# The low parts of the keys stacked twice, so that every score product contracts over 128 rows

## The chip, the cores and the metric

The kernel runs on one core of a Trainium2 chip, as one launch. The metric is the device time of one execution in microseconds. An execution's time is a little longer than its span in the trace, which goes from the first to the last instruction that was profiled.

## What is computed

The reference is two transformer blocks of two layers each, on 512 tokens of 1024 features, all in float32. The first block's layers have causal attentions with heads of 64 and a gated feed-forward; the second block's layers merge three branches (a global "axial" attention, a pooling branch and a neighbourhood attention) by gates, and have a feed-forward too. What the change touches is the product of queries and keys of the heads of 64:

```
s = q @ k.T / sqrt(64) + bias         # causal pairs, and both maps of the differential attention
s = [q_nope | q_rope] @ [k_nope | k_rope].T / sqrt(192)      # latent attention, rotated part of 64
s = einsum('bqhd,brqjhd->bhqrj', q_row, k_nb) + rpb          # neighbourhood attention
p = softmax(s);  o = p @ v
```

## The kernel before

Every float32 operand of a large product is split exactly into a high and a low part of a narrower type, and a product is summed from three: low times high, high times low, high times high (`mm3`, L356 to L360, nearly all of TensorE's work; the weights come from DRAM in chunks of 128x1024, through `Stream`).

For heads of 64 the split is arranged otherwise. Two heads lie in one tile, one in partitions 0 to 63 and one in 64 to 127. `stack` (L366) copies halves about by DMA, so that each head has one query tile with its high part above its low part, and one key tile with the high part of the keys in both halves. The low part of the keys stays as it was, one tile with a head in each half. `stacked` (L382) then gives two products per score tile: the query's high half times the low keys, which contracts over 64 rows (this text calls it a low product), and the whole query tile times the doubled high keys, which contracts over 128 rows:

```
        r = slice(64 * hd, 64 * hd + 64)
        q, kh, kl = store[hd], store[2 + hd], store[4]
        return [(q[r, c], kl[r, w]), (q[:, c], kh[:, w])]
```

`products` (L362, L364) issues them. They are used by the four pairs of causal heads and the four differential heads of the first layer ("even"), the four pairs and the rotated part of four latent heads of the second layer ("odd"), and the four pairs of the neighbourhood attention in each of the two layers of the second block. The axial attention has its own products (L1813, L1814), both over 128 rows, since its low keys are stored twice already.

Attention is a pipeline of units, a unit being at most a bank of scores: score products, then VectorE's sum with the bias and maximum (L629), ScalarE's exponential (L631), VectorE's scaling (L640, L642), TensorE's transposes (L654; L1832 in the neighbourhood attention), a copy, and the products with the values. `weave` (L531) mixes these units with dense work (projections, gates), and the framework then orders each engine's instructions by its own estimates; the order of the built program is fixed. All the tiles of 128x512 come from 42 blocks in SBUF. Guards on the number of free blocks hold work back: a neighbourhood unit is ready only with 6 free blocks (L1799), a gate of the last merge waits for 6 (L1660).

All the copies of `stack` and nearly all weight loads are issued from SyncE's queue, in order. A stack with keys issues six copies (three for the keys, three for the queries); the copy that overwrites a half waits there until the copies that read it have landed.

Of the kernel before, what the change touches and what calls it, by code (L numbers as in the profile page):

```python
# [10 lines left out]
F32R = mybir.dt.float32r  # L11
# [15 lines left out]
# the order of work in the pooling branch: gates, projections, mixing, products with the branch's weights  # L27
# [4 lines left out]
# ---------------------------------------------------------------- host layout  # L32
# [4 lines left out]
def weight_plan(I):  # L37
    """The weights in the order of their use: (key, scale, [128, n <= 1024])."""
# [145 lines left out]
def constants():  # L184
    """Arrays that follow from the shapes alone."""
    C = {}
    C["ident"] = np.eye(P, dtype=np.float32)
    # relative bias by reversed distance: column i stands for the distance 511 - i
# [35 lines left out]
    # pooling windows: 1 / count at the first and last eight tokens  # L224
# [5 lines left out]
    # neighbourhood windows, queries reversed within the tile: p = (15 - i) * 8 + (7 - r)  # L230
# [13 lines left out]
def rpb_layout(rpb):  # L244
    """[2, 8, 15, 31] as [2, 8, 16 shifts, 15 rows, 32 columns], zeros outside."""
    wide = np.zeros(rpb.shape[:3] + (48,), rpb.dtype)
    wide[..., 8:39] = rpb
    return np.ascontiguousarray(np.stack([wide[..., i:i + 32] for i in range(16)], axis=2))


# -------------------------------------------------------------------- program
class Blocks:
    """Slots of one size, handed out oldest-free first."""
# [19 lines left out]
class Stream:  # L273
    """Weights from DRAM, split exactly into two float32r parts some chunks ahead of their use."""
# [51 lines left out]
class Kernel:  # L326
# [8 lines left out]
    # ---- tiles  # L335
# [4 lines left out]
    def dbank(self):  # L340
        """A bank for dense work, in turn."""
# [13 lines left out]
    # ---- pieces  # L355
# [10 lines left out]
    def stack(self, qh, ql, kh=None, kl=None):  # L366
        """Two heads of 64, parts one above the other: per head, queries [high; low] and keys [high; high]."""
# [3 lines left out]
        if kh is not None:  # L371
            kb = self.blk.get(F32R)
            dma(kb[h], kh[g])
            dma(kb[g], kh[g])
            dma(kh[g], kh[h])
# [4 lines left out]
        return [qh, qb] if kh is None else [qh, qb, kh, kb, kl]  # L380

    def stacked(self, store, hd, c, w):  # L382
        r = slice(64 * hd, 64 * hd + 64)
        q, kh, kl = store[hd], store[2 + hd], store[4]
        return [(q[r, c], kl[r, w]), (q[:, c], kh[:, w])]

    def split(self, hi, lo, src):
        """src (float32, SBUF or PSUM) as the exact sum of two float32r parts."""
# [17 lines left out]
    # ---- pre-norm into the transposed, split hT  # L406
# [1506 lines left out]
```

## Time and profile before

| | before |
|---|---|
| time, median of 3 runs | 2935.75 us (2934.86 to 2935.95) |
| span of the profiled execution | 2933.1 us |
| around the span, from the median | 2.65 us |
| TensorE busy | 2878.6 us, 98% of the span, 13612 products |
| VectorE, ScalarE, GpSimdE busy | 1556.7, 1117.1, 125.2 us |
| DMA, mean of 16 engines | q1 (SyncE's and ScalarE's issues) 29.1% |

The profiled execution has no time of its own beside its span, so 2933.1 + 2.65 us stands for it, which is the median. Products are pipelined: two products of 512 columns start some 0.23 us apart though each is shown 0.39 us long, so a stretch is read by the starts, not by the busy time. A weight load (PEld) normally starts while the product before it streams.

### The profile page before, as it was taken

How to read it: one execution, taken by the hardware profiler on the slowest of the kernel's cores; microseconds unless marked ns; L12 is line 12 of the kernel's file. 1: busy time of each engine (PE TensorE's matmuls, PEld its weight loads, DVE VectorE, ACT ScalarE, POOL GpSimd, SP SyncE). 2: the span in 40 equal slices, each digit the busy share in tenths (PEclk: the TensorE clock that was granted, in tenths of full speed). 3: DMA queues.
4: the chain of work that ended last, by engine and by line, in shares of the span. 5: the costliest groups of instructions: out<-in, count | busy, mean ns of one | idle time of the engine just before them, and what ended most of it. 6: DMA issues, size and time to landing. Idle time of an engine off the chain costs nothing.

```text
span 2933.1 us, 34799 instructions
## 1 busy us (share of the span) xinstructions
PE 2878.6 (98%) x13612; PEld 2320.2 (79%) x13612; DVE 1556.7 (53%) x2673; ACT 1117.1 (38%) x1928; POOL 125.2 (4%) x206
## 2 busy tenths in 40 slices
PE   7999999999999999989999999999989999999999
PEld 6677888887678888777777888888867777888887
DVE  4566444335655443367556466652585554666533
ACT  3444333223433332234433344441444434444422
POOL 1000000000000000031000010000130000100000
PEclk9999999999999999999999999999999999999999
DMA  4432322333313223222223222233212222232232
GB/s 164 120 103 76 102 95 99 102 104 106 97 51 115 100 97 104 77 83 84 74 92 106 90 99 94 95 107 104 88 64 74 90 93 91 89 113 94 100 97 76
DMA packets 88849, 279.30 MB, mean 95 GB/s; under 512 B 11584, under 2 KB 14528, under 8 KB 88686
## 3 DMA queue, kind: packets, MB, share of 16 engines
q1 hardware_dynamic: 87726, 275.32, 29.1%
q8 instruction: 107, 1.75, 0.2%
q10 hardware_dynamic: 864, 1.64, 0.2%
q14 instruction: 56, 0.46, 0.0%
q0 software_dynamic: 96, 0.14, 0.0%
HBM read 258.38 MB, written 2.15 MB: 89 GB/s over the span
## 4 chain that ended last, share of the span: by engine, by line
PE 68%; issue 23%; DVE 5%; POOL 2%; DMA 1%; ACT 1%; SPq 0%; POOLq 0%; DVEq 0%; ACTq 0%
PE b L358 20%; PE b L359 20%; PE b L360 20%; PE b L364 2%; POOL s L403 1%; PE b L654 1%; PE b L1529 1%; DMA wr<-in_w_dram 1%; DVE k L1469 1%; PE b L1784 1%; POOL s L402 0%; PE b L1832 0%; PE b L1813 0%; DVE wl L301 0%; PE b L801 0%
## 5 line engine op out<-in xcount | busy, mean ns | idle before, releaser
L358 PE MATMUL b<-hh,wl 128*128 128x512 f32 (+1 forms) x2368 | 907.0, 384 | 1.8 <-ACT hh L389 1.0
L360 PE MATMUL b<-hh,wh 128*128 128x512 f32 (+1 forms) x2368 | 899.5, 380 | 0.0
L359 PE MATMUL b<-hl,wh 128*128 128x512 f32 (+1 forms) x2368 | 898.8, 380 | 0.0
L301 DVE TENSOR_TENSOR wl<-wr,wh 128x1024 fp32r<-128x1024 f32 (+1 forms) x407 | 495.9, 1221 | 530.8 <-ACT wh L300 529.0
L300 ACT CAST wh<-wr 128x1024 fp32r<-128x1024 f32 (+1 forms) x421 | 438.8, 1044 | 481.9 <-PE b L360 419.5
L358 PEld LDWEIGHTS b<-hh,wl 128*128 128x128 f32 x2368 | 446.1, 189 | 90.2 <-issue 10.6
L360 PEld LDWEIGHTS b<-hh,wh 128*128 128x128 f32 x2368 | 446.6, 189 | 83.4 <-issue 0.9
L359 PEld LDWEIGHTS b<-hl,wh 128*128 128x128 f32 x2368 | 447.1, 189 | 81.0 <-issue 3.2
L358 PE MATMUL b<-wh,k 128*128 128x512 f32 x900 | 352.9, 392 | 0.0
L359 PE MATMUL b<-wl,k 128*128 128x512 f32 x900 | 350.9, 390 | 0.0
L360 PE MATMUL b<-wh,k 128*128 128x512 f32 x900 | 350.5, 390 | 0.0
L358 PEld LDWEIGHTS b<-wh,k 128*128 128x128 f32 x900 | 169.1, 188 | 35.9 <-issue 0.8
L360 PEld LDWEIGHTS b<-wh,k 128*128 128x128 f32 x900 | 169.0, 188 | 35.6
L359 PEld LDWEIGHTS b<-wl,k 128*128 128x128 f32 x900 | 169.1, 188 | 33.9
L364 PE MATMUL b<-k,k 64*128 64x256 f32 (+9 forms) x400 | 128.3, 381 | 1.1 <-DMA k<-k 0.6
L1230 ACT ACTIVATE e<-b,cols_sb 128x512 f32<-128x512 f32 x88 | 68.4, 777 | 153.6 <-PE b L360 153.6
L364 PEld LDWEIGHTS b<-k,k 128*128 128x128 f32 (+1 forms) x400 | 71.1, 186 | 65.5 <-issue 33.3
L1231 DVE SCALAR_TENSOR_TENSOR e<-b,cols_sb,e 128x511 f32<-128x511 f32 x88 | 65.7, 747 | 104.5 <-ACT e L1230 104.3
L1220 DVE SCALAR_TENSOR_TENSOR e<-b,cols_sb,e 128x511 f32<-128x511 f32 x44 | 33.0, 750 | 159.2 <-ACT e L1219 159.2
L631 ACT ACTIVATE k<-k,s 128x256 f32<-128x256 f32 (+4 forms) x144 | 75.3, 524 | 72.1 <-DVE s L629 58.1
L1219 ACT ACTIVATE e<-b,cols_sb 128x512 f32<-128x512 f32 x44 | 34.3, 780 | 177.9 <-PE b L360 177.9
L359 PE MATMUL b<-wl,hh 128*128 128x512 f32 (+2 forms) x256 | 92.8, 362 | 0.4 <-DVE wl L301 0.3
(192 smaller groups left out, 3122.0 us busy)
## 6 DMA issues: line engine op xcount, KB each, us to landing
wr<-in_w_dram SPq DMA_DIRECT2D x451, 512.0 KB, 3.5
k<-k SPq DMA_DIRECT2D x126, 128.0 KB, 2.3
k<-brev SPq DMA_DIRECT2D x20, 256.0 KB, 3.3
x<-in_x_dram SPq DMA_DIRECT2D x4, 512.0 KB, 7.3
k<-in_rpb_dram SPq DMA_DIRECT2D x16, 128.0 KB, 2.7
wr<-in_w_dram SPq DMA_DIRECT2D x4, 448.0 KB, 3.2
e<-in_ffn_norm_dram SPq DMA_DIRECT2D x2, 512.0 KB, 3.7
e<-in_norm_mix_pre_dram SPq DMA_DIRECT2D x2, 512.0 KB, 4.4
```

The costliest lines, as they stand in the source:

```text
L300: nc.scalar.copy(hi[:, :n], raw[:, :n])
L301: (nc.gpsimd if self.pool > 0 else nc.vector).tensor_sub(lo[:, :n], raw[:, :n], hi[:, :n].bitcast(F32))
L358: mm(out, sl, mh, start=start, stop=False)
L359: mm(out, sh, ml, start=False, stop=False)
L360: mm(out, sh, mh, start=False, stop=stop)
L364: self.nc.tensor.matmul(out, s, m, start=i == 0, stop=i == len(pairs) - 1)
L403: nc.gpsimd.tensor_tensor(r, a, self.mhalf[:, :w], op=ALU.pow)
L631: nc.scalar.activation(s[:, c], s[:, c], AF.Exp, bias=mx[:, i:i + 1], scale=-1.0, accum_out=sm[:, i:i + 1])
L1219: nc.scalar.activation(c, b, AF.Identity, bias=self.col(("cb",), m), scale=self.col(("cw", 2), m))
L1220: nc.vector.scalar_tensor_tensor(c[:, 1:], b[:, :S - 1], self.col(("cw", 1), m), c[:, 1:], op0=ALU.mult, op1=ALU.add)
L1230: nc.scalar.activation(y, b, AF.Identity, bias=self.col(("cb",), mm), scale=self.col(("cw", 1), mm))
L1231: nc.vector.scalar_tensor_tensor(y[:, 1:], b[:, :S - 1], self.col(("cw", 0), mm), y[:, 1:], op0=ALU.mult, op1=ALU.add)
```

## The change

`stack` doubles the low parts of the keys as it does the high parts: one more block and three more copies for each stack with keys. `stacked` then multiplies the whole query tile, high over low, with the doubled low keys; the low-times-low term that was left out before is now in the sum. The number of products, their columns and all work of VectorE and ScalarE stay. Two guards follow: the last merge's gates wait for 7 free blocks, and a neighbourhood unit needs 6 free blocks only for the first unit of a pair, 2 for the others. Comments were dropped, which moves the line numbers by 3 below `stack`: L369 becomes L370, L654 becomes L657, L1529 L1532, L1832 L1835; L358 to L364 stay.

```diff
     def stack(self, qh, ql, kh=None, kl=None):
         h, g = slice(0, 64), slice(64, P)
         dma = lambda o, i: self.nc.sync.dma_start(o.bitcast(F32), i.bitcast(F32))
         qb = self.blk.get(F32R)
-        if kh is not None:
-            kb = self.blk.get(F32R)
-            dma(kb[h], kh[g])
-            dma(kb[g], kh[g])
-            dma(kh[g], kh[h])
+        keys = []
+        for part in (kh, kl):
+            if part is not None:
+                kb = self.blk.get(F32R)
+                dma(kb[h], part[g])
+                dma(kb[g], part[g])
+                dma(part[g], part[h])
+                keys.append((part, kb))
         dma(qb[g], qh[g])
         dma(qb[h], ql[g])
         dma(qh[g], ql[h])
         self.blk.put(ql)
-        return [qh, qb] if kh is None else [qh, qb, kh, kb, kl]
+        return [qh, qb] + [z for pair in keys for z in pair]
 
     def stacked(self, store, hd, c, w):
-        r = slice(64 * hd, 64 * hd + 64)
-        q, kh, kl = store[hd], store[2 + hd], store[4]
-        return [(q[r, c], kl[r, w]), (q[:, c], kh[:, w])]
+        q, kh, kl = store[hd], store[2 + hd], store[4 + hd]
+        return [(q[:, c], kl[:, w]), (q[:, c], kh[:, w])]
...
-                rope = k.stacked(mla["r", h // 2] + [cT[3][0], cT[3][0], cT[3][1]], h % 2, c, slice(0, n))
+                rope = k.stacked(mla["r", h // 2] + [cT[3][0]] * 2 + [cT[3][1]] * 2, h % 2, c, slice(0, n))
...
-            while len(k.blk.free) < 6:
+            while len(k.blk.free) < 7:
                 yield NEED
             yield from self.gate(L, 2, m)
...
-                     lambda: p in store and len(k.blk.free) >= 6, begin, tail)
+                     lambda: p in store and len(k.blk.free) >= (2 if tb else 6), begin, tail)
```

The change also moves instructions. The rows below are the built programs' order, without any time. Names are tiles with their numbers, `b` a bank of PSUM, `k` a block, `hh`/`hl` the parts of the normed activations, `wh`/`wl` those of the weights; shapes are those of the output.

TensorE, second pair of heads of the first layer, before: the low products (keys `k_716`) of the first two score tiles stand 27 rows higher, and the full products (`k_715`, the high keys) come one dense product into the next weight chunk.

```order
L360 MATMUL b_78_806<-hh,wh_515 128x512
L358 MATMUL b_79_841<-hh,wl_559 128x512
L364 MATMUL b_64_740<-k_715,k_643 128x512
L364 MATMUL b_69_758<-k_715,k_643 128x128
L364 MATMUL b_69_758<-k_716,k_643 128x384
L364 MATMUL b_69_758<-k_715,k_643 128x384
L359 MATMUL b_79_841<-hl,wh_558 128x512
```

The same place after the change (low keys `k_720`, high keys `k_719`):

```order
L358 MATMUL b_79_849<-hh,wl_563 128x512
L359 MATMUL b_79_849<-hl,wh_562 128x512
L364 MATMUL b_64_748<-k_720,k_647 128x512
L364 MATMUL b_64_748<-k_719,k_647 128x512
L364 MATMUL b_69_766<-k_720,k_647 128x128
L364 MATMUL b_69_766<-k_719,k_647 128x128
L364 MATMUL b_69_766<-k_720,k_647 128x384
L364 MATMUL b_69_766<-k_719,k_647 128x384
L360 MATMUL b_79_849<-hh,wh_562 128x512
```

The low products no longer stand ahead of the copies: low and full products stand together, 11 dense products into the next chunk instead of one.

SyncE's queue, the key copies of that same pair, before (each copy is 64x512; `x2` is two alike, `brev` is the bias table, `wr` a weight chunk):

```order
L763 DMA k_943<-brev 128x512
L763 DMA k_945<-brev 128x512
L369 DMA k_720<-k_715 64x512 x2
L286 DMA wr_804<-in_w_dram 128x1024
L369 DMA k_715<-k_715 64x512
```

And after:

```order
L370 DMA k_724<-k_719 64x512 x2
L370 DMA k_728<-k_720 64x512 x2
L766 DMA k_955<-brev 128x512
L370 DMA k_719<-k_719 64x512
L286 DMA wr_812<-in_w_dram 128x1024
L370 DMA k_720<-k_720 64x512
```

Two more copies stand before the one that completes the high keys, and one more, behind a weight load, completes the low keys.

TensorE, first pair of the neighbourhood attention in the second block's first layer, before: the first unit's scores (bank `b_989`) stand among the last axial work, and only dense work follows; the second unit's scores come some 120 rows later.

```order
L364 MATMUL b_989_11421<-k_11327,k_11251 128x256
L359 MATMUL b_997_11471<-hl,wh_11113 128x512
L364 MATMUL b_989_11421<-k_11326,k_11251 128x256
L364 MATMUL b_989_11421<-k_11327,k_11251 128x256
L654 MATMUL b_987_11398<-ident_sb,k_11356 128x128 x4
L364 MATMUL b_989_11421<-k_11326,k_11251 128x256
L654 MATMUL b_992_11433<-ident_sb,k_11373 128x128 x4
L360 MATMUL b_997_11471<-hh,wh_11113 128x512
L358 MATMUL b_997_11471<-hh,wl_11114 128x512
```

After, from the third unit's last score products to the first unit's transposes (the other products of the first three units stand just above):

```order
L364 MATMUL b_999_11516<-k_11383,k_11378 128x256
L364 MATMUL b_999_11516<-k_11379,k_11378 128x256
L360 MATMUL b_1011_11589<-hh,wh_11161 128x512
L358 MATMUL b_1011_11589<-hh,wl_11162 128x512
L359 MATMUL b_1011_11589<-hl,wh_11161 128x512
L657 MATMUL b_997_11506<-ident_sb,k_11443 128x128 x4
L364 MATMUL b_1005_11553<-k_11383,k_11378 128x192
L364 MATMUL b_1005_11553<-k_11379,k_11378 128x192
L1835 MATMUL b_1003_11541<-ident_sb,k_11474 128x128 x2
```

With the loosened guard three units' score products follow one another, and the fourth's begin before the first unit's transposes (`b_1003`); three dense products stand between.

## Rows read from the trace of the kernel before

**Rows 1.** Span and granted TensorE clock of the core.

```profile
core 0: 2933.1 us, clock 0.996
```

**Rows 2.** The page: busy time of each engine, share of the span, instructions.

```profile
PE 2878.6 (98%) x13612; PEld 2320.2 (79%) x13612; DVE 1556.7 (53%) x2673; ACT 1117.1 (38%) x1928; POOL 125.2 (4%) x206
```

**Rows 3.** Windows: stretch; length, busy us (instructions) per engine, clock, DMA share, GB/s.

```profile
78.00:272.00 194.00, 191.90 (x887) 137.37 (x886) 117.96 (x344) 82.26 (x225) 4.84 (x8) 1.00 0.34 96
...
690.00:870.00 180.00, 179.88 (x827) 130.46 (x826) 109.01 (x287) 78.44 (x190) 1.50 (x4) 1.00 0.30 85
...
1340.00:1473.00 133.00, 130.03 (x629) 99.23 (x629) 87.14 (x177) 62.47 (x126) 1.13 (x2) 1.00 0.25 78
1473.00:1640.00 167.00, 166.91 (x833) 127.59 (x832) 86.13 (x212) 62.79 (x133) 0.00 (x0) 1.00 0.31 95
```

**Rows 4.** Groups by form, weight loads of the score products: busy, mean ns, idle before.

```profile
L364 PEld LDWEIGHTS b<-k,k 128*128 128x128 f32 x224 | 39.8, 188 | 24.5 <-issue 10.1 <-ACT wh L303 1.0 <-ACT e L397 0.9
L364 PEld LDWEIGHTS b<-k,k 64*128 64x128 f32 x176 | 31.3, 183 | 41.0 <-issue 23.2 <-DVE s L640 2.9 <-DVE s L629 2.2
```

**Rows 5.** Timeline of TensorE, one low product among dense ones: start, length, instruction.

```profile
1602.17 0.39 PE L360 MATMUL b<-hh,wh 128*128 128x512 f32 x1
1602.49 0.38 PE L364 MATMUL b<-k,k 64*128 64x256 f32 x1
1602.80 0.50 PE L358 MATMUL b<-hh,wl 128*128 128x512 f32 x1
1603.14 0.40 PE L359 MATMUL b<-hl,wh 128*128 128x512 f32 x1
```

**Rows 6.** Timeline of TensorE, low and full products in turn, twice.

```profile
1614.66 0.40 PE L360 MATMUL b<-hh,wh 128*128 128x512 f32 x1
1614.99 1.21 PE L364 MATMUL b<-k,k 64*128 64x192 f32 x4
...
1616.29 0.39 PE L359 MATMUL b<-hl,wh 128*128 128x512 f32 x1
```

**Rows 7.** Timeline of TensorE, dense products of 256 columns.

```profile
290.23 0.28 PE L358 MATMUL b<-hh,wl 128*128 128x256 f32 x1
290.35 0.28 PE L359 MATMUL b<-hl,wh 128*128 128x256 f32 x1
```

**Rows 8.** Timeline of TensorE, an axial unit's two score products among dense ones.

```profile
1350.27 0.39 PE L1813 MATMUL b<-k,k 128*128 128x512 f32 x1
...
1350.73 0.39 PE L358 MATMUL b<-k,wl 128*128 128x512 f32 x1
```

**Rows 9.** Timeline of TensorE, low products that follow one another.

```profile
78.76 0.55 PE L364 MATMUL b<-k,k 64*128 64x512 f32 x2
...
185.60 0.50 PE L364 MATMUL b<-k,k 64*128 64x512 f32 x2
186.03 0.50 PE L359 MATMUL b<-hl,wh 128*128 128x512 f32 x1
...
2420.95 0.47 PE L364 MATMUL b<-k,k 64*128 64x256 f32 x2
```

**Rows 10.** The copies of L369: issues, who waited, issue to landing.

```profile
L369 SPq DMA_DIRECT2D k<-k x126: 461/462/946, 72.5 to 2440.8; - x126
...
  PE b L364: 0.6, 1
...
DMA to landing us min/median/max: 2.2/2.3/4.9
```

**Rows 11.** Groups by form, 1473 to 1640 us: VectorE's and ScalarE's steps of a unit.

```profile
L629 DVE CUSTOM_DVE_ANT_0 k<-b,k 128x256 f32<-128x256 f32 x16 | 6.2, 423 | 9.0 <-PE b L364 9.0
...
L642 DVE TENSOR_SCALAR k<-k,s 128x256 f32<-128x256 f32 x16 | 4.9, 350 | 0.2
...
L631 ACT ACTIVATE k<-k,s 128x256 f32<-128x256 f32 x16 | 8.1, 505 | 7.0 <-DVE s L629 7.0
...
L631 ACT ACTIVATION_READ_ACCUMULATOR k<-k,s 128x1 f32 x32 | 6.0, 188 | 0.0
```

## The prediction

> **What bounds the kernel now.** I read the page first: TensorE is busy 98% of the span, the other engines 53% and less [rows 2], at a granted clock of 0.996, its upper level of 2.4 GHz [rows 1]. Then the windows of the stretches that hold the score products [rows 3]: TensorE is busy 191.90 of 194, 179.88 of 180 and 166.91 of 167 us there (the second block's other layer, 2313 to 2480 us, repeats the last), while VectorE has 118, 109 and 86 us. So what TensorE is spared there shortens the kernel, as long as VectorE, ScalarE and the copies follow. A busy share hides whether TensorE streams or stands in a change of mode, so next come the starts in the timeline.
>
> Dense products of 512 columns start 0.23 us apart, and an axial unit's two products over 128 rows among them cost nothing extra: 1350.27 to 1350.73 us is two starts of 0.23 [rows 8]. A product of 256 columns takes 0.12 [rows 7]. A low product, over 64 rows, does cost extra. In [rows 5] the dense product before it is followed after 0.32 us in place of 0.23, the low product of 256 columns after 0.31 in place of 0.12, the next dense one after 0.34. From 1602.17 to 1603.14 is 0.97 us, where 0.23 + 0.12 + 0.23 = 0.58 would do: 0.39 us for one excursion to 64 rows and back. In [rows 6] two excursions stand in 1614.66 to 1616.29 = 1.63 us; with 0.12 for each of the four short products (they have 192 columns, so this is rather too much) and 0.23 for the two dense ones, 0.94 would do: 0.69 for two, 0.345 each. The weight load shows the same thing: before a low product the loader stood idle 41.0 us over 176 of them, most of it named "issue", which is no wait for another engine [rows 4].
>
> **What the change removes.** All 176 low products [rows 4] get 128 rows. Nine of them directly follow another low product (the first such pair is at 78.76, the last at 2420.95 us [rows 9]) and share its excursion, so 167 excursions go. At 0.345 to 0.39 us that is 57.6 to 65.1; I take 0.37, between the two, for 61.8 us. The products that replace them have the same columns, and their weight loads of 128 rows took 188 ns against 183 [rows 4], beside a streaming product: nothing.
>
> The Trainium skill's page "TensorEngine Tiling (Array Packing)", Key Properties, says that changing the tiling mode drains TensorE. The page "TensorE: Matmul & The Clock Gate", Single matmul latency, gives a product that hides no drain (398+N)/2.4 ns, so 166 ns above its columns; an excursion has two changes, and by that estimate the sum would be 167 x 0.332 = 55.4 us instead of 61.8.
>
> **What it adds: copies.** Each of the 20 stacks with keys (8, 4, 4 and 4) issues three more copies on SyncE's queue. An issue takes 0.46 us and a copy lands 2.2 to 4.9 us after it [rows 10]. They move no work of another engine, but the first low product of a pair now needs them, and weight loads queue behind. The order puts that first product 11 dense products into the next weight chunk, where the first full product stood one in: ten more, 2.3 us. The longer chain is one more issue pair (0.92 us) ahead of the last copy, and that last copy itself 0.46 us after its twin: 1.4 us, so the 2.3 us cover it if landing stays usual. TensorE waited for these copies 0.6 us, once [rows 10]. I take 0.1 us per stack, 2 us; the bounds are 0 and, if the last copy lands at 4.9 instead of 2.3 each time, 20 x 2.6 = 52 us. Weight loads late by some 1 to 2 us reach nobody: TensorE reads a chunk for 24 x 0.23 = 5.5 us and several chunks are prepared ahead; if that cover went, each stack would cost those 2 us, 40 in all, and TensorE would wait for a `wh`.
>
> **What it moves: the neighbourhood units.** With the looser guard three units of a pair stand together in the program, and the first one's transposes come after 8 short products of the next two units (0.96 us at 0.12), three dense ones (0.69), five transposes (below 0.12 each, 0.6) and two short products (0.24): 2.5 us after its scores. Its own chain takes at least: a sum with maximum 0.42, two exponentials with their accumulator reads 2 x (0.505 + 0.188) = 1.39, two scalings 0.70 [rows 11]: 2.5 us, and the four sums of the next two units (1.7 us) may stand before the scalings on VectorE: 4.2. So the first transposes wait 0 to 1.7 us, and the values' products and all dense work wait behind them on TensorE. Such packs of three come about twice more in each layer. I take 3.5 us per layer, 7 in all; bounds 0 and 3 x 2 x 1.7 = 10.
>
> **What is late next.** Each unit loses two excursions (0.74 us) of TensorE time that covered VectorE's and ScalarE's steps. How much of that comes back as waits is best read where there are no excursions: the axial stretch, with 32 units, leaves TensorE idle 133 - 130.03 = 3.0 us [rows 3], 0.09 per unit. For the 72 units of the other three attentions (24, 12, 24 and 12) that gives 6.7; they stall a little already, so I take 5. Bounds 0 and 72 x 0.3 = 22.
>
> **The sum.** 61.8 - 2 - 7 - 5 = 47.8 us less. The profiled execution's 2933.1 us and 2.65 around it are 2935.75, which is the median, since the former has no other time of its own: 2888 us. Its own range: 65.1 with no new wait gives 2871, 57.6 less all moderate losses (20) gives 2898.
>
> **Rivals.**
> *The softmax chain takes the place of the drains.* If VectorE and ScalarE, not TensorE, pace the attention stretches, most of what is freed comes back: 72 units at 0.3 us and 10 us in the neighbourhood stretches leave 61.8 - 22 - 10 - 2 = 28 us, 2908. For it: VectorE's share in the first stretch would go from 118 of 194 to 118 of some 170 us, 69% [rows 3]. Against: the axial stretch ran at 87 of 133, 66%, almost without waits. 12%.
> *The copies decide: slower.* The place is the first score product of a pair on TensorE, behind the last copy of the low keys; dense work stands behind it in order. With the other losses of 12 us it decides from (61.8 - 12) / 20 = 2.5 us of wait per stack. One round trip of 2.3 us [rows 10] that nothing covers would not do; two, 4.6 us, would cost 92 us in all and give 2935.75 + 92 - 61.8 + 12 = 2978. Against: the order moved the products by 2.3 us, and the copies of all but a pair's first use lie far ahead. 4%.
> *Side by side no more.* Low products of two heads use different halves of the rows and can run together: at 185.60 us two of 512 columns take 0.43 us to the next start, hardly more than one [rows 9]. If half of the 176 were hidden so, 88 x 0.17 (between 0.12 and 0.23) = 15 us of the gain would go, 2903. But only 2 pairs of the trace start together; low and full products alternate elsewhere. 4%.
> The Trainium skill's "TensorEngine Tiling (Array Packing)", Overview, promises up to twofold speed from two row tiles when the contraction is 64 or less, and so speaks against widening it; the trace shows the effect, in two places.
> *The change doesn't do what it says.* The surcharge might hang not on the rows but on the interruption of dense work; then nothing is gained and the waits remain, 2936 to 2945. [Rows 8] speak against it: the axial products interrupt dense work too, for nothing. 4%.
> My forecast keeps 76%.
>
> **How the numbers follow.** The likeliest gives 2888. The range goes from its lower end, 2871, rounded to 2870, up to take in the third rival and half of the first: 2905; some 2 in 10 is left out. A change of 0.2%, 6 us, is about what a measurement of this kernel can tell from none. Faster: the forecast, the first and third rivals and what little of the last could still gain, 93%. Same: the last one's milder half, 3%. Slower: the copies, and the last with its waits, 4%.
>
> **What would show it.** In the profile after, L364 has no 64-row form; starts around a lone score product are 0.23 and its own columns apart; the four stretches are shorter, the first by about 60 x 0.37 = 22 us, each neighbourhood stretch by about 11 less its waits; the axial stretches and the dense ones keep their length. If a step is wrong, it shows as idle TensorE: before L364 named by a copy (copies), before L657 or L1835 named by VectorE (chain), near 1480 and 2320 us (packs). I would be wrong altogether if the starts around score products kept their 0.31 to 0.34 us.

## The result and the profile after

| | before | after |
|---|---|---|
| time, median | 2935.39 us (2934.86 to 2935.95, 4 runs) | 2901.32 us (2897.02 to 2904.21, 4 runs) |
| ratio, with its 95% interval | | 0.9882 (0.9869 to 0.9894) |
| profiled execution, span | 2933.1 us | 2899.27 us, span 2897.2 us |

The change makes the kernel 34 us faster. The forecast was 48 us less, 2888 us, and its range of 2870 to 2905 us holds the result. In four runs each, the time after scatters over 7 us and that of before over 1. One of the four executions of experiment 6 below took 7301.66 us and counts as slow, so its median is that of the three others (the later expectations use 2885, the median of all four).

The span with the mean granted clock, and then the page's line of busy times (busy us, share of the span, instructions), of the kernel after, to be read beside [rows 1] and [rows 2]:

```profile
core 0: 2897.2 us, clock 0.995
```

```profile
PE 2829.7 (98%) x13612; PEld 2313.4 (80%) x13612; DVE 1551.5 (54%) x2673; ACT 1111.5 (38%) x1928; POOL 124.8 (4%) x206
```

TensorE has as many products as before and is busy 48.9 us less. The span is only 35.9 us shorter, so 13 us came back as TensorE standing still. The windows show in which stretches (columns as in [rows 3]):

```profile
78.00:264.00 186.00, 181.12 (x922) 140.29 (x921) 122.58 (x352) 83.33 (x231) 6.99 (x12) 1.00 0.42 118
...
670.00:850.00 180.00, 177.06 (x878) 137.92 (x878) 113.31 (x293) 79.85 (x194) 2.23 (x6) 1.00 0.35 100
1313.00:1446.00 133.00, 130.11 (x620) 99.25 (x619) 84.02 (x167) 61.13 (x123) 1.13 (x2) 0.99 0.24 77
1446.00:1612.00 166.00, 162.95 (x860) 130.31 (x859) 89.66 (x224) 64.64 (x136) 0.00 (x0) 1.00 0.36 106
```

In [rows 3] TensorE was idle 2.1 us in the first of them and 0.1 in the second and the last; now it is idle 4.9, 2.9 and 3.0. The axial stretch, which has no stacked score products, has 2.9 us as against 3.0. What ended the idle time is told by the weight loads of the score products (columns as in [rows 4]):

```profile
L364 PEld LDWEIGHTS b<-k,k 128*128 128x128 f32 x400 | 59.4, 189 | 25.2 <-DVE s L632 7.5 <-DMA k<-k 5.8 <-issue 3.1
```

The form with 64 rows is gone, and with it most of the idleness of "issue": in [rows 4] the loader stood 24.5 + 41.0 = 65.5 us before all 400 loads, here it stands 25.2. Two causes are new at the head: VectorE's maximum L632 (L629 before), and `DMA k<-k`, which is the copies of `stack`. They are seen from the other side too, in the view of the copies' line (min/median/max ns of an issue, first and last start; then who waited for the copies, in us and times):

```profile
L370 SPq DMA_DIRECT2D k<-k x186: 461/464/1798, 72.5 to 2408.3; - x186
...
  PEld b L364: 5.8, 7
  PE b L364: 4.2, 7
...
DMA to landing us min/median/max: 2.2/2.4/6.1
```

60 copies more, a slowest landing of 6.1 us in place of 4.9, and seven score products that wait for them where [rows 10] have one, for 0.6 us. One of these places is the second pair of heads, whose order in the program is shown under "The change". TensorE's timeline there (start, length, instruction, idle time of the engine and what ended it), and SyncE's issues just before:

```profile
102.65 0.39 PE L358 MATMUL b<-hh,wl 128*128 128x512 f32 x1
102.87 0.39 PE L359 MATMUL b<-hl,wh 128*128 128x512 f32 x1
104.20 1.30 PE L364 MATMUL b<-k,k 128*128 128x512 f32 x6 [0.94 <-DMA k<-k]
```

```profile
97.30 0.46 SPq L370 DMA_DIRECT2D k<-k  x1
97.86 0.53 SPq L286 DMA_DIRECT2D wr<-in_w_dram  x1
98.52 0.46 SPq L370 DMA_DIRECT2D k<-k  x1
99.03 0.59 SPq L766 DMA_DIRECT2D k<-brev  x1
```

The first score product should start 0.23 us after the dense one, at 103.10. It starts at 104.20, 5.7 us after the issue at 98.52 of the copy that completes the low keys; by the record of its landing this copy arrived at 104.2. Joined in this way for all copied blocks, by the program's order and the recorded landings, 13 blocks are first read within 0.25 us of their landing; before the change there were 7. At each of these places the gap between the starts of the read and of the product before it, less 0.23 us per 512 columns of the latter, is time in which TensorE stood: 8.0 us in all at the 13 places, and 2.0 us at the 7 before the change. The waits in the views are shorter, because each product is shown longer than it takes.

The steps of the forecast that went right show in the timeline around four short score products of 192 columns in the neighbourhood attention:

```profile
1589.63 0.39 PE L359 MATMUL b<-hl,wh 128*128 128x512 f32 x1
1589.86 0.40 PE L360 MATMUL b<-hh,wh 128*128 128x512 f32 x1
1590.09 0.58 PE L364 MATMUL b<-k,k 128*128 128x192 f32 x4
1590.52 0.41 PE L358 MATMUL b<-hh,wl 128*128 128x512 f32 x1
1590.77 0.39 PE L359 MATMUL b<-hl,wh 128*128 128x512 f32 x1
```

From the dense start at 1589.86 to that at 1590.77 are 0.91 us. The same six starts took 1.63 us with two excursions in them [rows 6], so each excursion cost 0.36 us in that place.

### The profile page after: what moved, and what is told of

Its sections match the earlier page's. It is cut to its first block, busy times and chain, and to the rows that moved or that the text cites. A ratio compares the mean times of both kernels' runs of the same rounds, so it can differ in the third digit from the quotient of the medians.

```text
span 2897.2 us, 34898 instructions
## 1 busy us (share of the span) xinstructions
PE 2829.7 (98%) x13612; PEld 2313.4 (80%) x13612; DVE 1551.5 (54%) x2673; ACT 1111.5 (38%) x1928; POOL 124.8 (4%) x206
## 4 chain that ended last, share of the span: by engine, by line
PE 64%; issue 25%; DVE 6%; POOL 2%; DMA 2%; ACT 1%; SPq 0%; POOLq 0%; DVEq 0%; ACTq 0%
PE b L358 19%; PE b L360 19%; PE b L359 19%; POOL s L406 1%; DMA k<-k 1%; PE b L657 1%; PE b L1532 1%; DMA wr<-in_w_dram 1%; DVE k L1472 1%; PE b L364 1%; DVE wl L301 1%; PE b L1787 1%; POOL s L405 1%; PE b L1835 0%; PE b L434 0%
## 5 line engine op out<-in xcount | busy, mean ns | idle before, releaser
L358 PE MATMUL b<-hh,wl 128*128 128x512 f32 (+1 forms) x2368 | 905.1, 383 | 1.8 <-ACT hh L392 1.0
L360 PE MATMUL b<-hh,wh 128*128 128x512 f32 (+1 forms) x2368 | 899.7, 380 | 0.0
L358 PEld LDWEIGHTS b<-hh,wl 128*128 128x128 f32 x2368 | 446.3, 189 | 90.6 <-issue 9.5
L360 PEld LDWEIGHTS b<-hh,wh 128*128 128x128 f32 x2368 | 446.9, 189 | 83.3 <-issue 1.4
L358 PE MATMUL b<-wh,k 128*128 128x512 f32 x900 | 352.8, 392 | 0.0
L360 PE MATMUL b<-wh,k 128*128 128x512 f32 x900 | 350.4, 390 | 0.0
L358 PEld LDWEIGHTS b<-wh,k 128*128 128x128 f32 x900 | 169.1, 188 | 35.7 <-issue 0.8
L360 PEld LDWEIGHTS b<-wh,k 128*128 128x128 f32 x900 | 169.0, 188 | 35.3
L358 PE MATMUL b<-wh,hl 128*128 128x512 f32 (+2 forms) x256 | 93.1, 364 | 0.0
L398 DVE COPY e<-b 128x512 f32<-128x512 f32 (+1 forms) x112 | 63.1, 564 | 54.8 <-PE b L1835 24.1
```

The costliest lines, as they stand in the source:

```text
L358: mm(out, sl, mh, start=start, stop=False)
L360: mm(out, sh, mh, start=False, stop=stop)
L398: self.nc.vector.tensor_copy(out, src)
```

## The experiments

All kernels were run beside the kernel before on the same chip; its medians there lie between 2935.2 and 2936.2 us. An excursion is, as in the forecast, the way from 128 rows to 64 and back. Two things had to be taken apart: what the excursions cost, and what the copies cost.

**1. Low products over 128 rows, without the added copies.** The kernel before with one line changed; the 128 rows then read the undoubled low keys.

```diff
-        return [(q[r, c], kl[r, w]), (q[:, c], kh[:, w])]
+        return [(q[:, c], kl[:, w]), (q[:, c], kh[:, w])]
```

> The kernel before with nothing but the low products over 128 rows: the low keys stay as they were, one tile with a head in each half, and no copy, block or guard is added. (Left out: the right value of the low term, since the query's low half now meets the other head's low keys; the time is that of the shapes.) If an excursion to 64 rows costs 0.335 us, as the trace of the changed kernel against the one before suggests, 167 of them are 56 us, and with some 4 us of new waits on the softmax chain this runs in about 2884 us; what the full change lost against that is then due to its copies and guards. Rival 1, the excursions cost only some 0.21 us and nothing was lost to new waits: about 2901, like the full change. Rival 2, VectorE and ScalarE pace the attention once the drains are gone: about 2900 too, with TensorE idle before transposes, named by VectorE.

Measured: 2893.66 us (2892.81 to 2895.13), ratio 0.9855 (0.984 to 0.9869). It lies between the expected values, 2884 and 2901. It is 7.7 us faster than the full change (the intervals of the two ratios leave 2 to 14 us), so the added copies, blocks and guards, and the order of products that comes with them, cost about that much together. Of its 400 score products, 396 stand behind the same dense product as in the kernel before, and its copies are those of that kernel. Yet TensorE now waits for them:

```profile
L369 SPq DMA_DIRECT2D k<-k x126: 461/462/917, 72.0 to 2400.7; - x126
...
  PE b L364: 7.5, 6
...
DMA to landing us min/median/max: 2.2/2.3/5.4
```

In [rows 10] the same row is 0.6 us, once. Taken from the starts, TensorE stands 10.3 us at the 10 places where a block is read within 0.25 us of its landing, in place of 2.0 at 7.

**2. The copies without the longer products.** The full change with the low products over 64 rows again.

```diff
+        r = slice(64 * hd, 64 * hd + 64)
         q, kh, kl = store[hd], store[2 + hd], store[4 + hd]
-        return [(q[:, c], kl[:, w]), (q[:, c], kh[:, w])]
+        return [(q[r, c], kl[r, w]), (q[:, c], kh[:, w])]
```

> The full change except that the low products still contract over 64 rows: the copies, the extra block and the guards alone. If the copies and guards are what the full change lost, and the drains do not cover their waits, this is slower than before by 10 to 20 us, 2945 to 2955, with TensorE waiting before score products for copies. If the excursions' own time hides the copies, within 6 us of before, 2935. If nothing was lost to copies and guards, 2935 as well, and then the first experiment decides.

Measured: 2939.07 us (2936.85 to 2941.37), ratio 1.0008 (0.9999 to 1.0018). Alone the copies cost 2.9 us by the medians, which can hardly be told from no change. Experiments 1 and 2 are no contradiction: the copies cost much only where the excursions are gone.

**3. Excursions put where there were none.** The kernel before, with the 64 low products of the axial attention cut to 64 rows (half of that term is left out).

```diff
-        nc.tensor.matmul(b, q, kl, start=True, stop=False)
+        nc.tensor.matmul(b, q[:64], kl[:64], start=True, stop=False)
```

> The kernel before with the axial attention's 64 low products cut to 64 rows (left out: the low keys times the low queries, which the axial products had). Nothing else changes: no copy, no block, no guard. It adds 64 excursions to stretches that have none, so it measures the price of one. At 0.335 us: plus 21, 2957. At the 0.37 of the prediction: plus 24, 2959. At 0.21 (rival 1): plus 13, 2949. If the interruption of dense work, not the rows, cost the time: 2935.

Measured: 2955.73 us (2955.45 to 2956.03), ratio 1.0065 (1.005 to 1.008): 19.5 us for 64 excursions, 0.305 each. The waits of the weight loader (us, times, longest) show on both sides of each excursion the idleness that is no wait for another engine:

```profile
PEld b L1813 <- issue: 17.1, 54, 0.4
...
PEld b L1814 <- issue: 15.2, 62, 0.2
```

The rows are the cause of the surcharge, and no interruption of dense work: these products stood in the same places in the kernel before, without it.

**4. The guards alone.** The kernel before with its two guards as in the change.

```diff
-            while len(k.blk.free) < 6:
+            while len(k.blk.free) < 7:
...
-                     lambda: p in store and len(k.blk.free) >= 6, begin, tail)
+                     lambda: p in store and len(k.blk.free) >= (2 if tb else 6), begin, tail)
```

> The kernel before with the two guards of the change and nothing else. If the packed neighbourhood units cost what the prediction took, 3.5 us per layer: 2942; if the drains between their products cover the packs: 2935 to 2938; if earlier units help: below 2935.

Measured: 2936.63 us (2935.48 to 2941.99), ratio 1.0003 (0.9993 to 1.0013): nothing, as long as the excursions are there.

**5. A stiffer neighbourhood guard in the full change.**

```diff
-                     lambda: p in store and len(k.blk.free) >= (2 if tb else 6), begin, tail)
+                     lambda: p in store and len(k.blk.free) >= (4 if tb else 6), begin, tail)
```

> The full change with the neighbourhood units' guard at 4 free blocks in place of 2, so that fewer units of a pair stand together. If the packs cost what the prediction took (3.5 us per layer), 2894 to 2898; if they cost little, as the guards alone did before the drains were gone, 2899 to 2903.

Measured: 2899.54 us (2896.55 to 2900.22), ratio 0.9873 (0.9856 to 0.9889), the same as the full change. The weight loader's waits before the score products, in that kernel:

```profile
PEld b L364 <- DMA k<-k: 7.3, 8, 1.6
PEld b L364 <- issue: 5.1, 5, 2.1
PEld b L364 <- DVE s L632: 4.3, 12, 0.6
```

The wait for VectorE's maximum fell from 7.5 to 4.3 us, and waits for copies and issue grew by as much. The edit moves only 24 of the 400 score products, by 23 to 34 dense products. What it takes apart of the packs of three units is worth less than can be told here, 1.8 us by the medians.

**6. No stack copies at all.** The full change with every copy of `stack` left out; the blocks are still taken, and both heads read the same tiles.

```diff
-                dma(kb[h], part[g])
-                dma(kb[g], part[g])
-                dma(part[g], part[h])
...
-        dma(qb[g], qh[g])
-        dma(qb[h], ql[g])
-        dma(qh[g], ql[h])
...
-        q, kh, kl = store[hd], store[2 + hd], store[4 + hd]
+        q, kh, kl = store[0], store[2], store[4]
```

> The full change with every copy of the stacks left out, the old ones too; the blocks that the copies would fill are still taken and given back, and both heads' products read the tiles that the projections wrote (left out: the copies, so that both heads are computed from one arrangement of queries and keys). The softmax chain is whole. If what the full change lost against its 51 to 56 us of spared excursions is the wait for copies, this gains nearly all of it: 2880 to 2886. If the loss is on the softmax chain, VectorE and ScalarE pacing the units, it stays: about 2895 to 2900.

Measured: 2884.36 us (2884.08 to 2885.71), ratio 0.9825 (0.9809 to 0.9842). That is 17 us less than the full change (the intervals leave 11 to 23) and 51 us less than before. But more than the copies is different: in the program's order 211 of the 400 score products stand behind an earlier dense product than in the full change, by up to 41 of them, and none behind a later one. So 17 us is the price of the copies together with the order that they bring.

**7. Low keys copied from GpSimdE's queue.**

```diff
-        for part in (kh, kl):
+        for part, dma in ((kh, dma), (kl, lambda o, i: self.nc.gpsimd.dma_start(o.bitcast(F32), i.bitcast(F32)))):
```

> The full change with the three copies of the low keys issued from GpSimdE's queue, which is nearly idle, in place of SyncE's. If the queue in order is what holds the low keys up (issues of 0.46 us each and weight loads between them), 2893 to 2898; if it is the two landings one after another, or if a transfer issued there starts later, no gain or a loss: 2901 to 2910.

Measured: 2924.52 us (2921.42 to 2926.53), ratio 0.996 (0.9945 to 0.9975), 23 us slower than the full change. That is outside both expectations. Its copies' line:

```profile
L373 POOL DMA_DIRECT2D k<-k x126: 516/516/713, 72.3 to 2432.4; - x126
...
  POOL k L373: 90.5, 33
  PE b L364: 16.8, 10
  PEld b L364: 9.6, 5
```

The copies land no later (median 2.5 us); but GpSimdE stands 90.5 us before the copies that must wait for others (33 times), and TensorE waits 16.8 us for copies in place of 4.2. Its mean clock is 0.992 in place of 0.995, which is some 9 us of 2924. These two come near the 23 us; that the one follows from the other was not tested.

**8. Copies into fresh blocks.** A third copy of each group overwrites a half that the copies before it read, so it waits on SyncE's queue for their landing, and the weights behind it wait too: in the full change 28 times, 20.5 us in all. Here both key tiles of a part are new blocks: four copies instead of three, none waiting for another.

```diff
-                kb = self.blk.get(F32R)
+                ka, kb = self.blk.get(F32R), self.blk.get(F32R)
                 dma(kb[h], part[g])
                 dma(kb[g], part[g])
-                dma(part[g], part[h])
-                keys.append((part, kb))
+                dma(ka[h], part[h])
+                dma(ka[g], part[h])
+                self.blk.put(part)
+                keys.append((ka, kb))
```

> The full change with the doubled keys copied into fresh blocks: four copies for each part in place of three, none of which has to wait for another copy to land (one more block while the stack is built). If the chain of copies with its wait in the middle (some 2.3 us on SyncE's queue) is what delays the first score product of a pair, this runs in 2892 to 2897; if the number of copies or their sharing of the transfers with weight loads is, it is no better than the full change or worse, 2901 to 2908.

Measured: 2893.23 us (2892.71 to 2895.7), ratio 0.9856 (0.9841 to 0.9871). 40 copies more than the full change, and 8 us faster. One block is read within 0.25 us of its landing in place of 13, and TensorE stands 0.4 us there in place of 8.0. At 12 of those 13 places the first score product stands within 4 dense products of where it stood, so it is the copies that land earlier and not the products that come later.

**9. Attention held back.** The full change, and then the kernel of experiment 8, with a stack's attention ready only six steps of the dense work after the stack.

```diff
+    def ripe(self, store, p):
+        if p not in store:
+            return False
+        at = self.made.setdefault((id(store), p), self.steps)
+        return self.blocked or self.steps - at >= 6
...
-            jobs.append(Job(k, Job.PAIR, self.heads64(store, p), tab(p), out, lambda p=p: p in store, begin(p),
+            jobs.append(Job(k, Job.PAIR, self.heads64(store, p), tab(p), out, lambda p=p: k.ripe(store, p), begin(p),
```

> The full change, and a stack's attention may begin only six steps of the dense work after the stack was issued, so that the two chains of copies have more time to land before the first score product. Theory (the full change loses about 16 us because first score products stand still for copies): most of that comes back, 2887 to 2893 us, and the trace has next to no idle weight load at the score products that is put down to keys' copies. Rival (the copies cost by the traffic on the queue or by pushing other transfers back, not by the first score product's wait): within 3 us of the full change, 2898 to 2904. Rival (attention that starts later leaves more of it uncovered at the ends of the stages, or meets the next stack): no gain or slower than the full change, 2900 to 2915.

> The doubled keys are copied into fresh blocks, so that no copy waits for another's landing (that alone took 2893 us), and attention begins only six dense steps after its stack. Theory: what copies still cost there (2893 against 2885 without any copies) goes as well, 2885 to 2889 us. Rival (the rest is the queue's traffic): 2892 to 2895. Rival (later attention costs at the stages' ends): 2895 or more.

Measured: 2906.45 us (2901.41 to 2910.66), ratio 0.9901 (0.9886 to 0.9916), and 2894.46 us (2892.47 to 2895.73), ratio 0.9862 (0.9846 to 0.9879). Neither gains, but neither is the test it was meant to be: in the order of the first one only 42 of the 400 score products stand behind another dense product than in the full change, 16 of them earlier, and all of them in the first layer. So it leaves open whether a real delay would help. In the second one no copied block is first read within 0.9 us of its landing, and that does not bring it below experiment 8. The trace of the first shows what a long wait for a copy costs, in the same pair of heads (windows of 2 us, columns as in [rows 3], then the timeline):

```profile
100.00:102.00 2.00, 1.25 (x6) 0.71 (x4) 0.69 (x1) 1.54 (x2) 0.00 (x0) 1.00 0.86 235
102.00:104.00 2.00, 0.21 (x1) 0.21 (x2) 0.00 (x0) 0.00 (x0) 0.00 (x0) 1.00 0.63 150
104.00:106.00 2.00, 2.00 (x10) 1.55 (x10) 1.44 (x3) 0.71 (x2) 0.00 (x0) 0.84 0.02 8
106.00:108.00 2.00, 2.00 (x6) 1.54 (x6) 2.00 (x11) 1.03 (x5) 0.00 (x0) 0.50 0.29 73
```

```profile
103.79 1.30 PE L365 MATMUL b<-k,k 128*128 128x512 f32 x6 [2.54 <-DMA k<-k]
...
106.32 0.63 PE L359 MATMUL b<-hh,wl 128*128 128x512 f32 x1
106.75 0.63 PE L360 MATMUL b<-hl,wh 128*128 128x512 f32 x1
```

TensorE stands 2.54 us for the copy, works again from 103.79, and between 104 and 106 us the granted clock falls to its lower level, 0.50: dense products start 0.43 us apart in place of 0.23.

**10. Excursions without copies.** The kernel of experiment 6 with the low products over 64 rows again.

```diff
+        r = slice(64 * hd, 64 * hd + 64)
         q, kh, kl = store[0], store[2], store[4]
-        return [(q[:, c], kl[:, w]), (q[:, c], kh[:, w])]
+        return [(q[r, c], kl[r, w]), (q[:, c], kh[:, w])]
```

> The kernel in which every stack copy is left out (2885 us with low products over 128 rows; both heads then read the same blocks), with the low products over the 64 rows of the head again. It gives the price of the excursions with no copy on the path: this time less 2885. Theory A (the excursions also hid the copies of the kernel before, so those cost nothing there): this is the time of the kernel before, 2933 to 2937 us, the 167 excursions cost 48 to 52 us, 0.29 to 0.31 each, and all that the full change lacks of this, some 16 us, is copies that no longer lie behind excursions. Theory B (copies cost the kernel before as well, about 8 us): 2925 to 2929 us, the excursions cost 40 to 44 us, and only some 8 us of the shortfall are the new copies. Theory C (the excursions are worth the 62 us of the forecast): 2945 us or more.

Measured: 2941.25 us (2936.48 to 2947.27), ratio 1.0019 (1.001 to 1.0029). Against experiment 6, which has every score product behind the same dense product, that is 57 us for 176 excursions (here none is shared), 0.32 each. Part of it is the clock, in each neighbourhood stretch (windows of 2 us of the first):

```profile
1600.00:1602.00 2.00, 2.00 (x10) 1.34 (x10) 1.65 (x7) 1.92 (x5) 0.00 (x0) 1.00 0.00 0
1602.00:1604.00 2.00, 2.00 (x8) 1.41 (x8) 1.39 (x8) 1.30 (x6) 0.00 (x0) 0.75 0.02 4
1604.00:1606.00 2.00, 2.00 (x7) 1.22 (x5) 1.51 (x8) 1.31 (x5) 0.00 (x0) 0.50 0.00 0
1606.00:1608.00 2.00, 2.00 (x6) 1.04 (x7) 0.51 (x4) 1.15 (x4) 0.00 (x0) 0.50 0.00 0
1608.00:1610.00 2.00, 2.00 (x9) 1.76 (x7) 0.91 (x4) 0.37 (x1) 0.00 (x0) 0.54 0.00 0
```

What is lacking of 1.00, times 2 us, is 3.4 us in these windows, and as much around 2430 us. The profiled executions, 2943.02 and 2884.08 us, lie 58.9 apart; without the two drops that is 52 us, 0.30 per excursion, as in experiment 3. It falls between theories A and C as they were put, and on A without the drops: theory B, that the copies cost the kernel before some 8 us, is out.

**11. Queries into fresh blocks too.** To experiment 8:

```diff
-        qb = self.blk.get(F32R)
+        qa, qb = self.blk.get(F32R), self.blk.get(F32R)
...
-        dma(qh[g], ql[h])
-        self.blk.put(ql)
-        return [qh, qb] + [z for pair in keys for z in pair]
+        dma(qa[h], qh[h])
+        dma(qa[g], ql[h])
+        self.blk.put(qh, ql)
+        return [qa, qb] + [z for pair in keys for z in pair]
```

> As the kernel with fresh blocks for the doubled keys (2893 us), and the queries are copied into fresh blocks too: no copy of a stack waits for another's landing. Theory (waits between copies are what the copies still cost there): 2887 to 2891 us. Rival (with no score product waiting for keys any more, what is left is the order of the program and the softmax): 2891 to 2896. Rival (one block more per stack holds up dense work): over 2896.

Measured: 2890.83 us (2890.26 to 2891.87), ratio 0.9846 (0.983 to 0.9863). Of the kernels here that leave nothing out it is the fastest: 45 us less than the kernel before (2935.97 in the same runs), 10 less than the full change, and it scatters over 1.6 us instead of 7. It lies at the edge between the theory and the first rival. What SyncE's queue waits for landings (us, times, longest), in the full change and then here:

```profile
SPq L370 <- DMA k<-k: 20.5, 28, 2.1
...
SPq L370 <- DMA k<-k: 0.3, 1, 0.3
```

Its copies' line, and the second pair of heads on SyncE's queue and on TensorE:

```profile
L370 SPq DMA_DIRECT2D k<-k x248: 461/588/1886, 71.7 to 2400.0; - x124
...
  DVE k L1764: 3.9, 2
  ACT k L1797: 0.8, 2
  DVE k L635: 0.4, 1
...
DMA to landing us min/median/max: 2.2/2.3/4.9
```

```profile
92.13 6.50 SPq L370 DMA_DIRECT2D k<-k  x8
98.73 0.52 SPq L286 DMA_DIRECT2D wr<-in_w_dram  x1
```

```profile
100.39 0.39 PE L358 MATMUL b<-hh,wl 128*128 128x512 f32 x1
100.62 1.19 PE L364 MATMUL b<-k,k 128*128 128x512 f32 x6
```

Eight copies leave back to back and no weight load gets between them, and the first score product starts 0.23 us after the dense one. No row of TensorE waits for a copy any more.

## Why the forecast was right, and which term was off

The 2x2 table of the runs holds most of the answer (medians, us):

| | all copies of the change | no copies at all |
|---|---|---|
| low products over 64 rows | 2939 (experiment 2) | 2941 (experiment 10) |
| low products over 128 rows | 2901 (the full change) | 2884 (experiment 6) |

In the right column the score products of both kernels stand behind the same dense products; in the left column, and from left to right, the order differs.

And the lengths of the stages, each measured between the starts of the same two dense products (L358 to L360, counted from the program's start) in every profiled execution; the rest is counted from the first product to the last:

| stage, dense products | before | after | fresh blocks (11) | no copies (6) |
|---|---|---|---|---|
| first layer's attentions, 255 to 725 | 191.5 | 176.6 | 171.9 | 169.8 |
| second layer's, 2660 to 3060 | 168.9 | 158.0 | 158.2 | 154.1 |
| axial, 5080 to 5500 and 8340 to 8740 | 281.9 | 284.5 | 284.9 | 283.7 |
| neighbourhood, 5500 to 6060 and 8740 to 9370 | 373.9 | 362.2 | 357.7 | 358.8 |
| all the rest | 1895.4 | 1894.2 | 1893.5 | 1894.2 |

**The mechanism: right.** The rows are the cause (experiment 3), the surcharge is gone from the timeline (0.91 for 1.63 us), and the gain lies in the stages named. The rival that nothing hangs on the rows is out. So are the rivals that the softmax chain paces the attentions (2908) and that products side by side are lost (2903): experiment 6 has the same chain and the same products and takes 2884. The rival of the copies names the right place, but wanted 2.5 us per stack, and at most a third of that came.

**Gross gain, 61.8 us from 0.37 per excursion: too large.** Experiment 3 gives 0.305 among products of 512 columns, so 167 x 0.305 = 51 us; experiment 10 gives 52 to 57 for its 176, which is 49 to 54 for 167. At the place of [rows 6] itself an excursion did cost 0.36, so the rows were read rightly, but they are the dear ones, around short products. The estimate that was set beside it, 55.4 us from the Trainium skill's "TensorE: Matmul & The Clock Gate" (Single matmul latency), lies nearer to what was measured than the sum from those rows.

**Packs 7 us and softmax chain 5 us: too dear.** Without copies the full change takes 2884.36, 51 us less than before. The forecast without its copy term was 49.8. As the gross gain is rather 49 to 54, and 2.0 us of standing for the old copies went too, all other losses are some 5 us at most and not 12; how these few divide into packs and chain was not measured. The new wait of 7.5 us before L364 for VectorE's L632 is the chain, but not in the place that was looked for: a score product waits until the maximum of an earlier unit has read its bank, as far as the names tell, while the forecast looked before the transposes, where VectorE is named for 0.5 us at L657 and at L1835 each. In experiment 6 this wait is still 5.8 us (8 times), and the gain is there all the same. These two errors cancelled the gross gain's, so that 49.8 comes so near to 51 is luck.

**Copies, 2 us: the term that failed.** The forecast took 0.1 us per stack, since "the order moved the products by 2.3 us" and the chain grew by 1.4 us. With the order that they bring, the copies cost 2901 - 2884 = 17 us, 0.8 per stack. Three sums of TensorE's standing, at the reads within 0.25 us of a landing, say how: 2.0 us in the kernel before, 10.3 in experiment 1, 8.0 in the full change. So the old copies, nearly free under the excursions, became dear when the excursions went, with the order all but unchanged; in the full change's order the added ones add nothing to that. It closes the account of experiment 1: 51 us of excursions less 8.3 of new standing is 42.7, and 2936.22 - 2893.66 = 42.6 was measured. The 0.6 us of [rows 10] was the cost under that cover. The first row of the 2x2 table agrees: with the excursions in place, all copies of the change cost 5 us at most (2939 against 2941, or against 2934 without the two drops of the clock). Two steps were wrong. The forecast priced the added copies alone, against a chain that it took to have slack, while 7 copied blocks were already being read within 0.25 us of landing; and it took the excursions' time to cover VectorE's and ScalarE's steps alone ("What is late next"), not the copies' landing.

What makes the copies late is that they wait for each other. Experiments 8 and 11 take these waits away (20.5 us on SyncE's queue, 0.3 in experiment 11), with more copies and more bytes. TensorE's standing falls from 8.0 to 0.4 and 0.2 us, and the time by 8.1 and 10.5 us; a price by traffic would have made them slower. That the weight chunk and the bias table issued between the copies (97.86 and 99.03 us) make the last one land 5.7 us after its issue instead of 2.4 is likely from the queue's rows, but was not tested by itself.

The rest of the 17 us, 6.5 from 2890.83 to 2884.36, is no wait of a score product for a copy: experiments 8, 11 and the second kernel of 9 have 0.4 us of that or less and take 2893, 2891 and 2894. It lies in the first two rows of the table of stages (2.1 and 4.1 us). The order of the program differs there, and whether that order is the cause stays open. So does whether later attention would help, since experiment 9 moved too little.

**The range.** The forecast's own range was 2871 to 2898, and 2901 lies outside it. The stated range holds the result by 4 us, because it was drawn up to 2905 for the third rival and half of the first. Neither of these came about; what came was a milder form of the second. To that extent the hit is luck.

**Stages.** Forecast: the first stretch 22 us shorter, each neighbourhood stretch 11 less its waits of 3.5, so 7.5. Measured: 14.9, and 5.9 on average. Without copies they are 21.7 and 7.6: the forecast's figures are those of a kernel without copies, stage by stage, with its two cancelling errors inside. The axial stages kept their length to 1%; of the 2.6 us that they grew together a part is the granted clock, 0.99 in the window of the first.

## What to carry to other kernels

When stalls are taken out of the engine that bounds a kernel, what finished just in time under them can be late next, transfers as much as engines: before pricing a new chain of copies, look at how far ahead of its first reader the old one lands, and not only at the waits that the trace names. A copy that overwrites what another copy reads holds its whole queue for a landing; a fresh block and one copy more was faster here (8 us, and 10.5 with the queries). And a price read from one place of the timeline holds for that place: short products made an excursion dearer (0.36 us) than long ones (0.305).

## What the hardware showed that was not expected

A wait of TensorE can cost more than its length, but need not. In experiment 9 the 2.54 us of standing for a copy were followed by a granted clock of 0.50 in which dense products started 0.43 us apart, between 104 and 110 us. In experiment 1 TensorE stood 2.80 us for a copy, until 1549.86, and the clock stayed at 1.00 through the windows up to 1558 us. In experiment 10 eight score products, low and full in turn from 1601 to 1604 us, all of it "busy" in the windows, stood ahead of the same drop, which lost 3.4 us there and again near 2430 us. In the full change's profiled execution the stretches of the pairs kept 1.00 in the windows above; its mean clock is 0.995, that of the first kernel of experiment 9, which stood longer, 0.993. The scatter of 7 us in the full change's times goes with the clock: the mean granted clock of its four executions is 0.996 (2897.02 us), 0.995 (2899.27) and twice 0.994 (2903.37 and 2904.21), and 0.002 of 2900 us is 6 us. Where the drops stood is not known, since only one execution has a trace. And the low keys' copies landed from GpSimdE's queue about as fast as from SyncE's (medians of 2.5 and 2.4 us), while the kernel took 23 us more: the transfer alone does not explain that, and the 90.5 us that copies stood in that queue for others may.
